# Eight of 22 gate and up pairs of four swiglu FFNs by seven half-size products, inner tiles in four groups

## The chip, the cores and the metric

One core of a Trainium2 chip runs the whole program. The metric is the device time of one execution in microseconds; the median of the runs is compared. TensorE (PE) multiplies, VectorE (DVE) and ScalarE (ACT) evacuate, round and combine, GpSimd (POOL) takes a few sums, and SyncE's queue (SP) starts the weight transfers.

## The reference

Two transformer blocks of 512 tokens and width 1024, in float32. The first block has two layers, and each layer has two swiglu FFNs, so there are four of them:

```
def swiglu(x, w_gate, w_up, w_down):
    return (jax.nn.silu(x @ w_gate) * (x @ w_up)) @ w_down

for i in range(DEPTH):                                  # DEPTH = 2
    h = rmsnorm(x, g_ffn1_pre[i])
    x = x + 0.5 * rmsnorm(swiglu(h, w1_gate[i], w1_up[i], w1_down[i]), g_ffn1_post[i])
    ...                                                 # attention mix
    h = rmsnorm(x, g_ffn2_pre[i])
    x = x + 0.5 * rmsnorm(swiglu(h, w2_gate[i], w2_up[i], w2_down[i]), g_ffn2_post[i])
    ...                                                 # gated projection ("ple")
```

The inner width is 2816, which is 22 tiles of 128. The second block (a recurrent mix, an FFN with a convolution, another gated projection) is not touched.

## The kernel before, in words

Activations lie transposed: a tile has 128 channels on the partitions and 512 tokens in its columns, and the width of 1024 makes eight such tiles (k = 0 to 7). Every product of float32 numbers is made of three matmuls: both operands are split into a high part (a copy rounded to float32r) and a low part (the rest), and `mm3` (L284 to L287) adds high x high, high x low and low x high in PSUM.

Weights arrive as raw buffers of up to 1024 columns, four of them in flight. `prep` (L138 to L150) makes the two parts of one unit: ACT casts 512 columns to `wh` (L146), and DVE subtracts to get `wl` (L147). `run` walks the list of steps that the builder wrote down; in front of each step it prepares at most one unit more, as long as fewer than `wu` units are prepared and not used up (8 in an FFN). So the order of instructions on every engine is fixed by that list, and each engine works through its own queue in order.

An FFN (`ffn`, L658) works inner tile by inner tile. The gate of tile n is eight `mm3` over all 512 tokens into one PSUM bank (24 matmuls of 512 columns), the up half the same into another bank. DVE multiplies each by the row of inverse norms (`act_gate` L681, `act_up` L706), ACT applies Silu (L683), DVE multiplies both (L712), and `split` makes the high and low part of the result, `dh` on ACT (L306) and `dl` on DVE (L307). The inner tiles are taken in pieces of 6, 8 and 8. After a piece the down projection runs over its tiles, for each of the eight output tiles (`pt` in PSUM), and its result is added to `f` (L779). Ahead of every piece but the first the gates of its first two tiles are computed before the down projection of the piece before, so that DVE can finish the last tile meanwhile.

The last piece has no such cover behind it. Its last four output tiles (`tail`) are computed in two halves of 256 tokens, and `boundary` (L501) threads the norm and the next sublayer's inputs through the second halves by a written plan: squares of the sum on ACT, sums over the partitions by PE transposes (`ss` L314), an inverse root on POOL (L323), a broadcast by PE (`bc` L330), then the update of x and the new `hh` and `hl`, with which the next sublayer's first matmuls (`hd` L638) start.

The lines that matter for the bank of a product are these:

```
def ps(self, s="o"):
    return self.pp.tile([P, T], F32, tag="ps", name=self.name(s))
```

A PSUM tile is one bank of 512 columns. Waits between engines are set for a tile as a whole, not for a range of its columns.

## Time and profile before

| what | value |
|---|---|
| three runs | 2878.39, 2880.08 (median) and 2880.47 us |
| profiled execution, its own time | 2879.94 us |
| its span in the trace | 2878.2 us |
| PE busy | 2850.8 us (99%) in 14942 matmuls |
| DVE busy | 1706.4 us (59%) |
| ACT busy | 1250.5 us (43%) |
| POOL busy | 216.9 us (8%) |
| chain that ended last | PE 88%, DVE 7%, ACT 4% |
| mean granted TensorE clock | 0.998 of full speed |
| DMA | 264.30 MB, mean 92 GB/s |

The time of an execution is 1.7 us longer than the span, which counts from the first to the last traced instruction. A busy PE is not PE at its peak: matmuls are pipelined, so the distance from one start to the next tells what one costs, not its duration. A group's row gives how often it ran, its busy time, the mean of one, and the idle time of the engine before it with what ended it.

### The profile page before, as it was taken

What the parts mean: (1) busy time and instruction counts of PE and PEld (TensorE: products, weight loads), DVE (VectorE), ACT (ScalarE), POOL (GpSimd) and SP (SyncE); (2) the same over time, 40 slices, a digit from 0 to 9 for tenths busy, and PEclk for the clock granted to TensorE, in tenths of its full rate; (3) what the DMA queues carried; (4) which work ended last, traced back from release to release, by engine and by line L of the source; (5) the groups of instructions that cost most, each with busy time, mean ns of one, the idle gap of its engine ahead of it and who ended that gap; (6) DMA issues with size and microseconds to landing.
All of it is one profiled execution on the core that took longest, in us unless ns stands there. A gap on an engine that the chain in (4) does not pass through costs nothing.

```text
span 2878.2 us, 38507 instructions
## 1 busy us (share of the span) xinstructions
PE 2850.8 (99%) x14942; PEld 2449.4 (85%) x14946; DVE 1706.4 (59%) x3048; ACT 1250.5 (43%) x2464; POOL 216.9 (8%) x252
## 2 busy tenths in 40 slices
PE   9999999999999999999999999999999999999999
PEld 8888898798888998888987898888988889888888
DVE  6454476865444595434668674434788746735458
ACT  5342347653322364322457653323546635433234
POOL 0000110010000220000111100000400001000013
PEclk9999999999999999999999999999999999999999
DMA  5333321123223223222121223233222222322320
GB/s 178 114 102 96 101 64 54 50 81 110 103 95 110 74 73 125 96 95 97 67 83 56 83 73 108 93 106 99 75 84 95 103 103 80 118 95 96 108 98 30
DMA packets 77750, 264.30 MB, mean 92 GB/s; under 512 B 9088, under 2 KB 11008, under 8 KB 77568
## 3 DMA queue, kind: packets, MB, share of 16 engines
q1 hardware_dynamic: 75600, 259.29, 27.3%
q0 software_dynamic: 1536, 2.10, 0.3%
q8 instruction: 118, 1.93, 0.3%
q10 hardware_dynamic: 432, 0.45, 0.1%
q14 instruction: 64, 0.52, 0.1%
HBM read 257.61 MB, written 2.10 MB: 90 GB/s over the span
## 4 chain that ended last, share of the span: by engine, by line
PE 88%; DVE 7%; ACT 4%; issue 1%; DMA 0%; POOL 0%; SPq 0%; DVEq 0%; ACTq 0%
PE gu L286 13%; PE gu L287 13%; PE gu L285 13%; PE hd L638 9%; PE pt L286 8%; PE pt L287 8%; PE pt L285 8%; PE in L285 3%; PE in L287 3%; PE in L286 3%; ACT p L1391 1%; DVE wl L147 1%; DVE ptl L307 1%; ACT wh L146 1%; DVE p L1400 1%
## 5 line engine op out<-in xcount | busy, mean ns | idle before, releaser
L147 DVE TENSOR_TENSOR wl<-raw,wh 128x512 fp32r<-128x512 f32 (+1 forms) x993 | 643.8, 692 | 149.0 <-ACT wh L146 144.9
L285 PE MATMUL gu<-hh,wh 128*128 128x512 f32 x1632 | 635.9, 390 | 0.0
L287 PE MATMUL gu<-hh,wl 128*128 128x512 f32 x1632 | 635.0, 389 | 0.0
L286 PE MATMUL gu<-hl,wh 128*128 128x512 f32 x1632 | 635.0, 389 | 0.0
L146 ACT CAST wh<-raw 128x512 fp32r<-128x512 f32 (+1 forms) x993 | 545.2, 605 | 202.3 <-PE pt L286 98.2
L285 PE MATMUL pt<-dh,wh 128*128 128x512 f32 (+1 forms) x1056 | 377.7, 358 | 0.0
L286 PE MATMUL pt<-dl,wh 128*128 128x512 f32 (+1 forms) x1056 | 376.9, 357 | 0.0
L287 PE MATMUL pt<-dh,wl 128*128 128x512 f32 (+1 forms) x1056 | 376.8, 357 | 0.0
L287 PEld LDWEIGHTS gu<-hh,wl 128*128 128x128 f32 x1632 | 306.4, 188 | 63.6
L285 PEld LDWEIGHTS gu<-hh,wh 128*128 128x128 f32 x1632 | 306.4, 188 | 63.3
L286 PEld LDWEIGHTS gu<-hl,wh 128*128 128x128 f32 x1632 | 306.4, 188 | 63.2
L306 ACT CAST dh<-ur 128x512 fp32r<-128x512 f32 x112 | 69.5, 620 | 463.1 <-DVE ur L712 463.1
L655 POOL TENSOR_TENSOR acc<-acc,sq 128x256 f32<-128x256 f32 (+1 forms) x96 | 99.6, 1037 | 1916.8 <-ACT sq L653 1916.2
L286 PEld LDWEIGHTS pt<-dl,wh 128*128 128x128 f32 x1056 | 199.6, 189 | 28.9
L285 PEld LDWEIGHTS pt<-dh,wh 128*128 128x128 f32 x1056 | 199.5, 189 | 29.0
L287 PEld LDWEIGHTS pt<-dh,wl 128*128 128x128 f32 x1056 | 199.5, 189 | 28.5
L706 DVE TENSOR_TENSOR ur<-gu,rb 128x512 f32<-128x512 f32 x102 | 70.4, 690 | 253.2 <-PE gu L287 253.2
L779 DVE TENSOR_TENSOR f<-pt,f 128x512 f32<-128x512 f32 (+1 forms) x100 | 58.3, 583 | 237.4 <-PE pt L287 237.3
L285 PE MATMUL in<-hh,wh 128*128 128x512 f32 x432 | 170.6, 395 | 3.9 <-DVE ptl L307 2.3
L638 PE MATMUL hd<-hh,wh 128*128 128x256 f32 (+1 forms) x672 | 170.1, 292 | 0.4 <-ACT hh L464 0.4
L287 PE MATMUL in<-hh,wl 128*128 128x512 f32 x432 | 168.4, 390 | 0.0
L286 PE MATMUL in<-hl,wh 128*128 128x512 f32 x432 | 168.3, 390 | 0.0
(396 smaller groups left out, 4448.4 us busy)
## 6 DMA issues: line engine op xcount, KB each, us to landing
raw<-in_w_dram SPq DMA_DIRECT2D x449, 512.0 KB, 3.3
raw<-in_w_dram SPq DMA_DIRECT2D x36, 384.0 KB, 3.1
x<-in_x_dram SPq DMA_DIRECT2D x8, 256.0 KB, 6.5
raw<-in_w_dram SPq DMA_DIRECT2D x4, 432.0 KB, 3.6
pt<-in_p_dram SPq DMA_DIRECT2D x6, 256.0 KB, 4.0
out_dram<-pgt SPq DMA_DIRECT2D x10, 128.0 KB, 1.7
qh<-qrh POOLq DMA_DIRECT2D x16, 64.0 KB, 1.9
ql<-qrl POOLq DMA_DIRECT2D x16, 64.0 KB, 2.0
```

What stands on the lines that cost most here:

```text
L146: self.S.copy(h, src)
L147: self.low.append((u, lambda h=h, l=l, src=src: self.V.tensor_sub(l, src, h.bitcast(F32))))
L285: self.E.matmul(o, lh, rh, start=start, stop=False, **kw)
L286: self.E.matmul(o, lh, rl, start=False, stop=False, **kw)
L287: self.E.matmul(o, ll, rh, start=False, stop=stop, **kw)
L306: self.S.copy(hi, src)
L307: self.V.tensor_sub(lo, src, hi.bitcast(F32))
L638: self.E.matmul(q, w, h, start=k == 0 and j == 0, stop=k == KD - 1 and j == 2)
L655: eng.tensor_tensor(sub.acc[:, t0:t1], sub.acc[:, t0:t1], sq[:, t0:t1], op=ALU.add)
L706: V.tensor_mul(ur[:, t0:t1], ou, sub.rb[:, t0:t1])
L779: V.tensor_tensor(f, q, f, op=ALU.add)
L1391: S.activation(s.p[t][:, c : c + n], s.sc[t][:, c : c + n], AF.Exp, bias=mx[qb], accum_out=s.sum[:, qb : qb + 1])
```

## The change

In each of the four swiglu FFNs the inner tiles 8 to 11 and 14 to 17 are computed in another way, and the pieces are 6, 6, 6 and 4 tiles instead of 6, 8 and 8. The FFN of the second block stays as it was.

For such a tile the gate weights, the up weights and the normalised input are cut into 2 x 2 blocks: the weights by the upper and lower 512 channels and by gate and up, the input by the upper and lower channels and by tokens 0 to 255 and 256 to 511. Strassen's identity (in Winograd's form) needs seven products of these blocks instead of eight. Each product is four `mm3` over 256 tokens, 12 matmuls of 256 columns.

- Four combinations of the input (`token_sums`, once for each of four channel pairs of an FFN) are made by ACT and DVE during the first piece and kept in 16 tiles.
- Four combinations of the weights are made for each tile by DVE (`prep_part`, lines with q1 to q4), and then rounded and split as other weights are. A tile has four parts: part 0 holds blocks 11 and q1, part 1 holds 12 and q2, part 2 holds q4 and q3, part 3 holds 22. The limit `wu` is 5 parts or units from tile 4 on until tile 18.
- The products go into two banks, `r` (both halves of its columns) and `r3` (one half). `seven_run` writes the steps of a group of four tiles. For tile n they are: two products into `r` (part 0); ACT's copy of `r` (`s15`); a product into `r3` (part 1); then, for the tile before, its last product (part 3) and the steps that finish it; a second product into the first half of `r` (part 1); ACT's copy of that half (`s2`); a product into the second half of `r` (part 2); DVE's addition, scaling and Silu of the gate; another product into the first half of `r` (part 2); DVE's up half.

The first two tiles of a piece stay as they were, and so do their early gates. Cut to its core the diff is:

```diff
-WU_TAIL, WU_SB, WU_MLA = 10, 6, 6
+WU_TAIL, WU_SB, WU_MLA, WU_SEVEN = 10, 6, 6, 5
+SEVEN = (8, 9, 10, 11, 14, 15, 16, 17)
...
+    def prep_part(self, u):
+        q = u.quad
+        ra, rb = (r.tile for r in q.raws)
+        w = {"22": ra[:, 0:T], "11": ra[:, T:], "12": rb[:, 0:T], "21": rb[:, T:]}
+        low = []
+        def add(key, a, b):
+            q.q[key] = self.a("q")
+            self.V.tensor_add(q.q[key], a, b)
+        def put(key, src):
+            h, l = u.blocks[key] = (self.a("wh", F32R), self.a("wl", F32R))
+            self.S.copy(h, src)
+            low.append(lambda: self.V.tensor_sub(l, src, h.bitcast(F32)))
+        if u.j == 0:
+            put("11", w["11"])
+            add("q1", w["21"], w["22"])
+            put("q1", q.q["q1"])
+        elif u.j == 1:
+            put("12", w["12"])
+            add("q2", q.q.pop("q1"), w["11"])
+            put("q2", q.q["q2"])
+        elif u.j == 2:
+            add("q4", q.q.pop("q2"), w["12"])
+            put("q4", q.q.pop("q4"))
+            add("q3", w["11"], w["21"])
+            put("q3", q.q.pop("q3"))
+        else:
+            put("22", w["22"])
...
+        def token_sums(k):
+            g1, g2, x1, x2 = sub.gpre(k), sub.gpre(k + 4), self.X[k], self.X[k + 4]
...
+        def product(o, part, block, key, start):
+            h, l = part.blocks[block]
+            for k in range(4):
+                c = slice(k * P, (k + 1) * P)
+                self.mm3(o, h[:, c], l[:, c], *operand(key, k), start and k == 0, k == 3, skip=True)
...
+            def last(st, n):
+                step(lambda: product(st.r[:, A], st.u[3], "22", "t4", False), [st.u[3]], mm=True)
+                def out():
+                    gr, ur = raw.pop(n)
+                    V.scalar_tensor_tensor(ur[:, A], st.r[:, A], -1.0, gr[:, A], op0=ALU.mult, op1=ALU.mult)
+                    V.tensor_mul(ur[:, B], ur[:, B], gr[:, B])
+                    hid[n] = (self.a("dh", F32R), self.a("dl", F32R))
+                    self.split(ur, *hid[n])
+                    st.r = None
+                step(out)
...
+                def one(st=st):
+                    st.r, st.r3 = self.ps("gu"), self.ps("gu")
+                    product(st.r[:, A], st.u[0], "11", "11", True)
+                    product(st.r[:, B], st.u[0], "q1", "t1", False)
...
+                def gate_b(st=st, n=n):
+                    gr = pair(n)[0]
+                    V.tensor_tensor(gr[:, B], st.r[:, B], st.s2[:, A], op=ALU.add)
+                    V.tensor_mul(gr, gr, sub.rb)
+                    S.activation(gr, gr, AF.Silu)
+                    self.later.append(lambda: V.tensor_mul(gr, gr, sub.rb))
...
+                step(one, [st.u[0]], mm=True)
+                step(copy)
+                step(lambda st=st: product(st.r3[:, A], st.u[1], "12", "21", True), [st.u[1]], mm=True)
+                if prev:
+                    last(*prev)
+                step(lambda st=st: product(st.r[:, A], st.u[1], "q2", "t2", False), [st.u[1]], mm=True)
+                step(two)
+                step(gate_a)
+                step(lambda st=st: product(st.r[:, B], st.u[2], "q4", "22", False), [st.u[2]], mm=True)
+                step(gate_b)
+                step(lambda st=st: product(st.r[:, A], st.u[2], "q3", "t3", False), [st.u[2]], mm=True)
+                step(up_b)
+                prev = (st, n)
+            last(*prev)
...
-                self.ffn(..., (6, 8, 8), 4.0 / D, 4.0 * EPS, first=L == 0)
+                self.ffn(..., (6, 6, 6, 4), 4.0 / D, 4.0 * EPS, first=L == 0, seven=SEVEN)
```

In the functions `copy` and `two`, left out above, ACT copies `st.r` to `st.s` and its first half to `st.s2`; `gate_a` is DVE's addition of `st.r3` and `st.s`, and `up_b` its subtraction for the second half of the up product.

How the order of instructions moves is shown at three places of the first layer's first FFN. The first is DVE at a tile inside the second group. Before, tile 16 (`gr`, `ur`: its gate and up half; `rb`: the inverse norms) takes these rows on DVE:

```order
L681 TENSOR_TENSOR gr_2259<-gu_2193,rb_483 128x512 [waits PE_49]
L147 TENSOR_TENSOR wl_2254<-raw_2109,wh_2253 128x512 [waits DMAHW5_49,Activation_49]
L147 TENSOR_TENSOR wl_2257<-raw_2109,wh_2256 128x512 [waits Activation_49]
L681 TENSOR_TENSOR gr_2267<-gu_2224,rb_483 128x512 [waits PE_49]
L706 TENSOR_TENSOR ur_2260<-gu_2271,rb_483 128x512 [waits PE_49]
L147 TENSOR_TENSOR wl_2297<-raw_2147,wh_2296 128x512 [waits DMAHW6_49,Activation_49]
L147 TENSOR_TENSOR wl_2300<-raw_2147,wh_2299 128x512 [waits Activation_49]
L712 TENSOR_TENSOR ur_2260<-ur_2260,gr_2259 128x512 [waits DVE_49]
L307 TENSOR_TENSOR dl_2303<-ur_2260,dh_2302 128x512 [waits Activation_49]
```

The banks `gu` are read once each, and the weights prepared in between come straight from raw buffers. The same place with the change, from the finish of tile 14 (`ur_2354`) to the gate of tile 15 (`gr_2497`), with `q` the combinations of weights for tile 16:

```order
L863 SCALAR_TENSOR_TENSOR ur_2354<-gu_2279,gr_2353 128x256 [waits PE_49]
L864 TENSOR_TENSOR ur_2354<-ur_2354,gr_2353 128x256
L371 TENSOR_TENSOR dl_2463<-ur_2354,dh_2462 128x512 [waits Activation_49]
L167 TENSOR_TENSOR wl_2458<-raw_2071,wh_2457 128x512
L162 TENSOR_TENSOR q_2481<-q_2424,raw_2311 128x512
L162 TENSOR_TENSOR q_2486<-raw_2195,raw_2311 128x512
L167 TENSOR_TENSOR wl_2484<-q_2481,wh_2483 128x512 [waits Activation_49]
L167 TENSOR_TENSOR wl_2489<-q_2486,wh_2488 128x512 [waits Activation_49]
L890 TENSOR_TENSOR gr_2497<-gu_2396,s_502_2429 128x256
L894 TENSOR_TENSOR gr_2497<-gu_2395,s_514_2491 128x256 [waits PE_49,Activation_49]
L895 TENSOR_TENSOR gr_2497<-gr_2497,rb_483 128x512 [waits DVE_49]
L897 TENSOR_TENSOR gr_2497<-gr_2497,rb_483 128x512 [waits Activation_49]
```

The two combinations for tile 16 (L162) now stand behind the finish of tile 14 (L863), which waits for PE. The second place is ACT at the same tile, from the copy of `r` (L883) to the Silu of tile 15:

```order
L883 COPY s_502_2429<-gu_2395 128x512 [waits PE_49]
L166 CAST wh_2457<-raw_2071 128x512
L370 CAST dh_2462<-ur_2354 128x512 [waits DVE_49,Activation_49]
L166 CAST wh_2483<-q_2481 128x512 [waits DVE_49,Activation_49]
L166 CAST wh_2488<-q_2486 128x512 [waits DVE_49]
L887 COPY s_514_2491<-gu_2395 128x256 [waits PE_49]
L896 ACTIVATE gr_2497<-gr_2497 128x512 [waits DVE_49]
```

Before, ACT had only casts from raw buffers, one `dh` and one Silu in a tile. Now the copy L887 of tile 15 stands behind two casts for tile 16 that wait for DVE. The third place is PE at the same tile, where the product of q2 into `r` (`gu_2395`) ends and the product of q4 into its other half begins:

```order
L350 MATMUL gu_2395<-ts_808,wh_2268 128x256
L351 MATMUL gu_2395<-ts_807,wl_2269 128x256
L349 MATMUL gu_2395<-hh_244,wh_2339 128x256 [waits Activation_49]
L350 MATMUL gu_2395<-hl_245,wh_2339 128x256
L351 MATMUL gu_2395<-hh_244,wl_2340 128x256
```

Before, the 24 matmuls of a gate followed each other with waits only for their weights. Now the product of q4 starts with a wait for ACT, and twelve rows further the product of q3, the next one into `gu_2395`, starts with a wait for DVE. By the counts in the built program the first is that of the copy L887 and the second that of DVE's addition L894.

## Rows read from the trace of the kernel before

**Rows 1.** Page, part 1 and part 4: busy time of each engine, shares of the last chain.
```profile
PE 2850.8 (99%) x14942; PEld 2449.4 (85%) x14946; DVE 1706.4 (59%) x3048; ACT 1250.5 (43%) x2464; POOL 216.9 (8%) x252
...
PE 88%; DVE 7%; ACT 4%; issue 1%; DMA 0%; POOL 0%; SPq 0%; DVEq 0%; ACTq 0%
```

**Rows 2.** Busy time by stretch, first FFN: start:end, length, PE, PEld, DVE, ACT, POOL, clock, DMA.
```profile
60.00:330.00 270.00, 270.00 (x1193) 223.64 (x1192) 134.09 (x228) 87.75 (x159) 1.36 (x5) 1.00 0.34 103
```

**Rows 3.** Timeline, PE: start, duration, line, product; gate matmuls of 512 columns.
```profile
300.05 0.39 PE L286 MATMUL gu<-hl,wh 128*128 128x512 f32 x1
...
302.77 0.39 PE L286 MATMUL gu<-hl,wh 128*128 128x512 f32 x1
```

**Rows 4.** Timeline: down matmuls of 256 columns, and DVE's addition behind one.
```profile
351.77 0.28 PE L285 MATMUL pt<-dh,wh 128*128 128x256 f32 x1
...
358.13 0.28 PE L287 MATMUL pt<-dh,wl 128*128 128x256 f32 x1
...
358.45 0.42 DVE L779 TENSOR_TENSOR f<-pt,f 128x256 f32<-128x256 f32 x1 [2.46 <-PE pt L287]
...
361.01 0.28 PE L287 MATMUL pt<-dh,wl 128*128 128x256 f32 x1
```

**Rows 5.** Timeline, DVE and ACT around one up half of the third FFN piece.
```profile
807.39 0.69 DVE L706 TENSOR_TENSOR ur<-gu,rb 128x512 f32<-128x512 f32 x1 [4.75 <-PE gu L287]
808.00 1.28 DVE L147 TENSOR_TENSOR wl<-raw,wh 128x512 fp32r<-128x512 f32 x2
809.20 0.68 DVE L712 TENSOR_TENSOR ur<-ur,gr 128x512 f32<-128x512 f32 x1
809.97 0.62 ACT L306 CAST dh<-ur 128x512 fp32r<-128x512 f32 x1 [5.64 <-DVE ur L712]
810.50 1.14 ACT L146 CAST wh<-raw 128x512 fp32r<-128x512 f32 x2
810.62 0.69 DVE L307 TENSOR_TENSOR dl<-ur,dh 128x512 fp32r<-128x512 f32 x1 [0.74 <-ACT dh L306]
```

**Rows 6.** Groups by line and shape, whole span: count, busy us, mean ns.
```profile
L560 DVE TENSOR_TENSOR accx<-accx,sq 128x512 f32<-128x512 f32 x49 | 33.9, 691 | 4.4
...
L683 ACT ACTIVATE gr<-gr 128x512 f32<-128x512 f32 x88 | 55.1, 632 | 189.8 <-DVE gr L681 189.7
...
L777 ACT COPY f<-pt 128x512 f32<-128x512 f32 x40 | 23.5, 587 | 102.6 <-PE pt L287 102.6
...
L821 ACT COPY f<-pt 128x256 f32<-128x256 f32 x24 | 8.8, 366 | 24.3 <-PE pt L287 24.3
```

**Rows 7.** Timeline, boundary behind the first FFN: from the last first-half product to the next matmuls.
```profile
361.13 0.38 PE L314 MATMUL ss<-ident,acc 128*128 128x128 f32 x2
...
366.49 0.48 DVE L538 SCALAR_TENSOR_TENSOR t<-f,cols,sb 128x256 f32<-128x256 f32 x1 [0.43 <-ACT sb L523]
...
367.53 0.51 ACT L540 ACTIVATE hh<-x,cols 128x256 fp32r<-128x256 f32 x1 [1.07 <-DVE x L539]
...
374.32 0.51 ACT L540 ACTIVATE hh<-x,cols 128x256 fp32r<-128x256 f32 x1 [1.78 <-DVE x L539]
```

**Rows 8.** Timeline, PE: two waits of PE in the attention of layers 2 and 1.
```profile
1616.12 0.27 PE L287 MATMUL yv<-pth,vl 128*128 128x128 f32 x1
1618.44 0.69 PE L285 MATMUL part<-yh,wh 128*128 128x512 f32 x1 [2.04 <-ACT p L1391]
...
1621.92 0.43 PE L287 MATMUL part<-yh,wl 128*128 128x512 f32 x1
...
574.42 0.50 PE L285 MATMUL part<-yh,wh 128*128 128x512 f32 x1 [1.98 <-ACT p L1391]
574.76 0.39 PE L286 MATMUL part<-yl,wh 128*128 128x512 f32 x1
```

**Rows 9.** Busy time by stretch around the first wait of rows 8; the clock stands third from the end.
```profile
1619.00:1620.00 1.00, 1.00 (x4) 0.81 (x3) 0.18 (x2) 1.00 (x5) 0.00 (x0) 0.50 0.00 0
```

More of the change, by code (lines that the diff above doesn't have):

```diff
@@ L74, in __init__ @@
         self.lo = lambda k: units[k].lo(0)[:, c]
+class Quad:
+    def __init__(self, hosts):
+        self.hosts, self.raws, self.q = hosts, None, {}
+        self.parts = [Part(self, j) for j in range(4)]
+class Part:
+    n, dims = 1024, (8, P)
+    def __init__(self, quad, j):
+        self.quad, self.j, self.blocks = quad, j, {}
 class Raw:
@@ L135, in cols_units @@
         return [Unit(lambda inp, c=c: host(inp, c), (kn, width)) for c in range(c0, c0 + ncol, width)]
+    def prep_part(self, u):
[25 more added lines that the diff above has]
+            put("22", w["22"])
+        self.low.append((u, lambda: [f() for f in low]))
     def prep(self, u):
+        if isinstance(u, Part):
+            return self.prep_part(u)
         kn, w = u.dims
@@ L209, in run @@
         for u in order:
+            if isinstance(u, Part):
+                if u.quad.raws is None:
+                    u.quad.raws = [Raw(), Raw()]
+                    for r, host in zip(u.quad.raws, u.quad.hosts):
+                        block = Unit(host, (8, P))
+                        block.at, r.units, r.n = 0, [block], RAW
+                    raws.extend(u.quad.raws)
+                u.raw = u.quad.raws[1]
+                continue
             if len(raws) < 3 or raws[-1].n + u.n > RAW:
@@ L216, in run @@
             r.left = sum(-(-u.dims[0] // (T // u.dims[1])) for u in r.units)
+        for u in order:
+            if isinstance(u, Part):
+                u.quad.raws[0].left, u.quad.raws[1].left = 4, 3
         self.declare(raws)
@@ L241, in flush_low @@
                     f()
-                    u.raw.left -= 1
-                    if u.raw.left == 0:
-                        self.rlive -= 1
+                    for r in (u.quad.raws[: 2 if u.j < 3 else 1] if isinstance(u, Part) else [u.raw]):
+                        r.left -= 1
+                        if r.left == 0:
+                            self.rlive -= 1
                 else:
@@ L740, in ffn @@
         self.plain_head(sub, head, evac)
+        sums = {}
+        A, B = slice(0, T // 2), slice(T // 2, T)
+        def token_sums(k):
+            g1, g2, x1, x2 = sub.gpre(k), sub.gpre(k + 4), self.X[k], self.X[k + 4]
+            xg, a, b = self.a("xg"), self.a("ta"), self.a("tb")
+            S.activation(xg, x1, AF.Copy, scale=g1)
+            V.tensor_sub(a[:, A], xg[:, A], xg[:, B])
+            V.scalar_tensor_tensor(a[:, B], x2[:, B], g2, xg[:, B], op0=ALU.mult, op1=ALU.subtract)
+            V.scalar_tensor_tensor(b[:, A], x2[:, B], g2, a[:, A], op0=ALU.mult, op1=ALU.add)
+            V.scalar_tensor_tensor(b[:, B], x2[:, A], g2, b[:, A], op0=ALU.mult, op1=ALU.subtract)
+            ah, al, bh, bl = (self.a("ts", F32R) for _ in range(4))
+            self.split(a, ah, al)
+            S.activation(bh, b, AF.Copy, scale=-1.0)
+            V.scalar_tensor_tensor(bl, b, -1.0, bh.bitcast(F32), op0=ALU.mult, op1=ALU.subtract)
+            sums[k] = (ah, al, bh, bl)
@@ new lines, in operand @@
+        def operand(key, k):
+            if key in ("11", "21", "22"):
+                hh, hl = sub.h[k + 4 * (key[0] == "2")]
+                c = A if key[1] == "1" else B
+            else:
+                i = 0 if key in ("t1", "t3") else 2
+                hh, hl = sums[k][i : i + 2]
+                c = A if key in ("t1", "t2") else B
+            return hh[:, c], hl[:, c]
+        def product(o, part, block, key, start):
[3 more added lines that the diff above has]
+                self.mm3(o, h[:, c], l[:, c], *operand(key, k), start and k == 0, k == 3, skip=True)
@@ L751, in body @@
                         self.step(ahead[1])
+                    if seven and n == 4:
+                        wu, self.wu = self.wu, WU_SEVEN
+                    if seven and n > seven[-1]:
+                        self.wu = wu
+                    if n in seven:
+                        if n - 1 not in seven:
+                            seven_run([i for i in seven if n <= i < n0 + kn])
+                        continue
                     if n not in early:
@@ L755, in body @@
                         self.both(item(i, 1))
+                        if seven and pc == 0:
+                            self.step(lambda k=i - 2: token_sums(k))
                 if not final:
```

32 lines of the change are left out of this document (29 added, 3 removed).

## The prediction

> **What bounds the kernel now.** I read the page first: PE is busy for 99% of the span and holds 88% of the chain that ended last, with DVE at 59% and ACT at 43% [rows 1]. Then the stretch that the change rewrites: from 60 to 330 us, inside the first FFN, PE is busy for all of 270 us at full clock, DVE for 134 and ACT for 88 [rows 2]. There PE waits for nobody, so time is won only by fewer or cheaper matmuls, and lost by any wait of PE that nothing covers. The third view is the timeline, for what one matmul costs from start to start. Twelve starts with 512 columns take 302.77 - 300.05 = 2.72 us, 226.7 ns each [rows 3]. With 256 columns 77 starts take 361.01 - 351.77 = 9.24 us, 120.0 ns each [rows 4]. Half the columns cost 53%, not 50%.
>
> **What the products save.** A gate and up pair took 48 matmuls of 512 columns, 48 x 226.7 ns = 10.88 us. Now it takes 84 of 256 columns, 84 x 120.0 ns = 10.08 us. That is 0.80 us, on 8 tiles of 4 FFNs: 32 x 0.80 = 25.7 us. Of eight products one is saved, 12.5%, but the shorter matmul gives 5 points of it back. The last piece of 4 tiles instead of 8 also turns 96 down matmuls of 256 columns into 48 of 512 in each FFN: 96 x 0.120 - 48 x 0.2267 = 0.64 us, 2.6 us in four. Together 28 us. The order agrees with the count: 32 x 36 matmuls more and 4 x 48 fewer make the 960 by which PE's rows grew, so the change does what it says.
>
> By the Trainium skill, "TensorE: Matmul & The Clock Gate", section "Back-to-back issue gap", the distance at full clock is columns / 2.4 plus 2.5 ns, 215.8 and 109.2 ns here; an estimate by that page would save 1.19 us in a pair, 38 us in all instead of 25.7. The trace differs from it, and its 120.0 ns decide.
>
> **What the products cost: waits of PE.** Before, a bank was filled, read once and left. Now bank `r` is filled in five products with reads between them. Two of these reads have nothing between them and the next product into `r`: PE's product of q4 waits for ACT's copy L887, which reads the product just before it, and PE's product of q3 waits for DVE's addition L894, which reads q4's. I walk a tile in the middle of a group, with PE's last product of the tile before ending at 0.
>
> - DVE starts 0.20 us behind the last issue slot of a product (358.13 + 0.12 to 358.45 [rows 4]). DVE's rows of 512 columns follow each other 0.60 us apart and last 0.69, ACT's casts 0.52 apart and last 0.62, and between engines 0.03 to 0.09 pass (all [rows 5]); I take 0.05.
> - L863 runs from 0.20 (0.48 for a three-operand row of 256 columns [rows 7]), L864 from 0.60 to 1.02, `dh` on ACT from 1.07 to 1.69, `dl` from 1.74, `wl` from 2.34, the two sums of weights L162 from 2.94 to 3.63 and 3.54 to 4.23 (0.69 as for other f32 additions [rows 6]).
> - ACT casts q4 from 3.68 to 4.30 and q3 from 4.28 to 4.90, and only then comes the copy L887: 4.80 to 5.17 (0.37 for 256 columns out of PSUM [rows 6]). PE may begin the product of q4 at 5.22. It was done with the product of q2 at 1.44. It waits 3.8 us.
> - Behind q4's product DVE's L894 takes 0.20 + 0.42 + 0.05 = 0.67 us, and PE waits that long for q3.
> - A first matmul behind a wait costs 0.34 us to the next start instead of 0.23 [rows 8]: 0.11, twice.
>
> That makes 4.7 us in a middle tile. From the end of q3's product PE has 5.8 us of products that wait for nothing late, in which DVE (14 rows of 512 and 5 of 256 columns in a tile, 10.4 us) and ACT catch up, so the next tile begins as this one did. A group has two such tiles. In its first tile nothing has to be finished before the sums, but the tile before it still has its split to do; the same walk gives 1.0 for the copy, 0.67 for L894 and three restarts, 2.0 us. In its last tile the casts behind it are of plain weights and need no sums: 1.4 for the copy, 0.9 for L894, and 1.1 more because the last product into `r` follows q3's at once and waits for DVE's up half (sum, scaling, Silu of 0.63 [rows 6], scaling, L900); with restarts 3.7. A group costs 2.0 + 2 x 4.7 + 3.7 = 15.1 us, eight groups 121 us.
>
> The bank is the unit of these waits. The Trainium skill, "PSUM — Partial Sum Buffer", section "PSUM bank collisions raise a hardware error", asks that PSUM be guarded by bank and quadrant rather than by address. By that rule q4's product, which goes to the half that the copy does not read, must wait all the same, as in the sum; guarded by address it would start at 1.44, q3 would wait until 5.22 instead, 2.3 us, and eight groups would cost about 33 us less. No run here shows it.
>
> **The clock.** Behind a wait of 2.04 us in the attention of the second layer eight starts took 1621.92 - 1618.44 = 3.48 us instead of 1.81 [rows 8], at a granted clock of 0.50, the 1.2 GHz level [rows 9]. A wait of 1.98 us in the first layer, with the next start 0.34 us on [rows 8], did not bring it down. Waits of 3.8 us are longer than either, so I count the lower level once for each middle tile, 3.48 - 1.81 - 0.11 = 1.6 us: 16 x 1.6 = 26 us. Bounds: nothing, and the lower level all through the middle tiles (below).
>
> **The last piece.** With four tiles instead of eight its down product reaches the newest `dl` after 10 matmuls, 2.3 us, instead of 22, 5.0 us. From the end of the up half to the end of that `dl` it takes 811.31 - 807.19 = 4.1 us [rows 5], so PE waits 1.9 us that were covered, 7.6 in four FFNs. The second halves that cover the boundary shrink from 8 x 1.44 = 11.5 us to 5.8. From the end of the first halves (358.25) to the first `hh` (368.04) 9.8 us pass [rows 4, 7], part of them spent on waiting for a slot on PE; the sixth `hh` then comes 6.8 us behind the first [rows 7], where PE would want it after 4.8. The cost is between 0 and 5 us a boundary. I take 2, since the slots come earlier too and two of the four have a projection's products as cover: 8 us. Together 16 us, bounds 6 and 28.
>
> **Costed at nothing.** The four `token_sums` of an FFN (3.2 us of DVE each) and the eight more additions to `f` lie in stretches where DVE is busy half the time and weights are prepared five units of 5.4 us ahead; without that cover they would be some 13 us an FFN. A tile's weights still are two transfers of a raw buffer; the buffer of part 3 comes free some 6 us ahead of its next use, and if it came late, the sums L162 would.
>
> **The sum.** 121 + 26 + 16 - 28 = 135 us on the profiled execution's own 2879.9 us (the median of the runs, 2880.08, is the same): **3014 us**.
>
> **Rivals.**
> - *The clock holds.* The waits come as walked, and the trace's wait of 1.98 us without a fall is the rule: 3014 - 26 = 2988 us. 22%.
> - *Bare round trips.* ACT and DVE run ahead, so no copy stands behind a late cast. Then a tile costs 0.62 (0.20 + 0.37 + 0.05) + 0.67 + 0.22 = 1.5 us, 32 of them 48, and the group's last wait 8 x 1.1 = 9: 48 + 9 + 16 - 28 = +45, 2925 us. DVE's 50% in rows 2 speaks for it, the place of L162 behind L863 in its queue against it. 10%.
> - *The clock stays low* in the middle tiles. A matmul then costs 0.43 instead of 0.23 [rows 8], half of the difference with 256 columns: 84 x 0.1 = 8.4 us a tile, 16 x 8.4 = 134 instead of 26: 3122 us. PE is busy two thirds of such a tile, which speaks against it. 6%.
> - *Faster: PE does not wait at q4 and q3.* If the two waits there are met early (by casts done a tile ahead, not by L887 and L894), the columns decide: 16 - 28 = -12, 2868 us. The point is 0.80 us a tile: with less than that for both waits the change wins. The bare round trips alone are 1.5, and the built program's counts are those of L887 and L894. 4%.
>
> **How the numbers follow.** The forecast holds 56%, and 2% lie near no change. A measurement of this kernel can tell about 0.2%, 6 us, from nothing. Faster by more than that 0.04, within it 0.02, slower 0.94. The range takes in the forecast with its bounds (walked waits 15% shorter or longer, 18 us; the last piece 6 to 28; the clock in the first and last tiles too, 26 more) and the case without the clock, and reaches to the upper part of the bare round trips: 2935 to 3070.
>
> **What would show it.** Right: PE in the groups has idle time ended by ACT's copy L887, over 3 us in two tiles of a group, and by DVE's L894, about 0.7 in each; the distance of 256-column matmuls stays at 120 ns at full clock; the clock of a group's stretch is below 1. Wrong: no PE wait on L887 over 1 us, or PE busy through the groups. The forecast fails most easily in the size of the wait before q4, 16 times 3.8 us.

## The result and the profile after

The kernel with the change takes **3057.29 us** (median of 4 runs, 3055.04 to 3063.58), against 2880.27 us before on the same chip: a ratio of **1.0621**, 95% interval 1.0608 to 1.0635. That is 177 us slower, where 134 were predicted; it lies inside the range of 2935 to 3070. The profiled execution of the change has a span of 3056.9 us.

The page of the kernel after, parts 1 and 4 (the lines that answer to [rows 1]), and the clock of part 2 by slices of 76 us:

```profile
PE 2892.4 (95%) x15902; PEld 2519.0 (82%) x15906; DVE 1956.2 (64%) x3560; ACT 1369.0 (45%) x2704; POOL 218.3 (7%) x252
...
PEclk9889999999998999999999999998999999999999
...
PE 79%; DVE 13%; ACT 6%; issue 2%; POOL 0%; DMA 0%; ACTq 0%; DVEq 0%; SPq 0%; POOLq 0%
```

PE has fallen from 99% to 95% busy and from 88% to 79% of the last chain; DVE and ACT took the difference. No engine has become the busiest in PE's place: PE stands still for them in places. The view of waits, PE alone (line, what it waited for, us in total, times, longest), says where:

```profile
PE gu L349 <- ACT s L887: 75.5, 32, 3.6
PE gu L349 <- DVE gr L894: 20.2, 32, 0.9
PE gu L349 <- ACT s L883: 19.1, 1, 19.1
PE ss L378 <- DVE acc L719: 6.3, 4, 1.6
PE gu L349 <- DVE ur L900: 6.1, 8, 0.8
```

Four of these lines are the groups' own: 75.5 + 20.2 + 19.1 + 6.1 = 120.9 us. The first two and L900 were forecast; the third, one wait of 19.1 us, was not. Now the timeline around the beginning of the product of q4 in a middle tile (start, duration, engine, line):

```profile
284.74 0.42 DVE L863 SCALAR_TENSOR_TENSOR ur<-gu,gr 128x256 f32<-128x256 f32 x1 [1.26 <-PE gu L351]
285.59 0.62 ACT L370 CAST dh<-ur 128x512 fp32r<-128x512 f32 x1 [1.83 <-DVE ur L864]
...
285.86 0.28 PE L351 MATMUL gu<-ts,wl 128*128 128x256 f32 x1
...
287.45 0.68 DVE L162 TENSOR_TENSOR q<-q,raw 128x512 f32<-128x512 f32 x1
288.05 0.69 DVE L162 TENSOR_TENSOR q<-raw,raw 128x512 f32<-128x512 f32 x1
288.22 1.17 ACT L166 CAST wh<-q 128x512 fp32r<-128x512 f32 x2 [2.02 <-DVE q L162]
...
289.30 0.37 ACT L887 COPY s<-gu 128x256 f32<-128x256 f32 x1
289.71 0.58 PE L349 MATMUL gu<-hh,wh 128*128 128x256 f32 x1 [3.58 <-ACT s L887]
...
293.23 0.58 PE L349 MATMUL gu<-ts,wh 128*128 128x256 f32 x1 [0.59 <-DVE gr L894]
```

This is the chain of the prediction, row by row: PE waits for a copy of 0.37 us that needs nothing but PE's product of q2, and that copy stands in ACT's queue behind two casts of weight sums, which wait 2.02 us for DVE's additions L162, which stand in DVE's queue behind the previous tile's L863, `dl` and `wl`.

Busy time by stretch (start:end, length, the engines, then the clock third from the end): three of the eight groups, from the first product of a group to its last.

```profile
128.10:213.60 85.50, 51.25 (x337) 48.82 (x336) 56.06 (x104) 28.82 (x52) 0.00 (x0) 0.76 0.18 57
268.30:329.70 61.40, 49.08 (x336) 46.88 (x335) 39.06 (x70) 22.99 (x44) 0.00 (x0) 0.86 0.23 75
1935.00:1992.50 57.50, 45.16 (x336) 43.10 (x336) 39.03 (x70) 22.90 (x44) 0.00 (x0) 0.94 0.25 81
```

The other five groups last 61.1, 61.1, 60.5, 60.2 and 61.1 us; all eight last 508.4, and 510.3 from each group's first matmul to the end of its last issue slot (these windows begin up to 0.3 us late). Their products alone, 8 x 28 x 1.44 us, are 322.6, and the four plain tiles that stood there before were 8 x 4 x 10.88 = 348.2. So the groups cost 510.3 - 348.2 = 162 us net, and 187.7 us over their products. Counted over the starts of PE's matmuls in the trace, these are:

- 120.9 us in 73 waits as listed above.
- 14 us around these waits that the view does not list. It counts a wait from the end of the matmul before, 0.28 us behind that one's start (the row at 285.86), where the next start could have come after 0.12 (both are more at the low clock).
- 11 us of restarts: the first start behind a wait is further from the next than usual.
- 41 us of low clock: 450 starts at a granted clock of 0.50, the 1.2 GHz level, lie 0.21 us apart instead of 0.12.

Smaller differences make up the last 1 us. The remaining 17 of the 178.7 us by which the spans differ lie outside the groups; a run below gives them to the short last piece.

### The profile page after: what moved, and what is told of

The parts are those of the page before. It is cut to its first block, busy times and chain, and to the rows that moved or that the text cites. A ratio compares the mean times of both kernels' runs of the same rounds, so it can differ in the third digit from the quotient of the medians.

```text
span 3056.9 us, 41198 instructions
## 1 busy us (share of the span) xinstructions
PE 2892.4 (95%) x15902; PEld 2519.0 (82%) x15906; DVE 1956.2 (64%) x3560; ACT 1369.0 (45%) x2704; POOL 218.3 (7%) x252
## 4 chain that ended last, share of the span: by engine, by line
PE 79%; DVE 13%; ACT 6%; issue 2%; POOL 0%; DMA 0%; ACTq 0%; DVEq 0%; SPq 0%; POOLq 0%
PE gu L349 12%; PE gu L351 11%; PE gu L350 11%; PE hd L702 8%; PE pt L350 7%; PE pt L351 7%; PE pt L349 7%; PE in L349 3%; PE in L351 3%; PE in L350 3%; DVE wl L198 2%; ACT wh L166 1%; ACT p L1576 1%; DVE wl L167 1%; ACT dh L370 1%
## 5 line engine op out<-in xcount | busy, mean ns | idle before, releaser
L198 DVE TENSOR_TENSOR wl<-raw,wh 128x512 fp32r<-128x512 f32 (+2 forms) x897 | 564.9, 674 | 114.9 <-ACT wh L197 111.0
L349 PE MATMUL gu<-hh,wh 128*128 128x512 f32 (+1 forms) x1504 | 561.3, 373 | 75.5 <-ACT s L887 75.5
L197 ACT CAST wh<-raw 128x512 fp32r<-128x512 f32 (+2 forms) x897 | 477.9, 588 | 181.3 <-DMA raw<-in_w_dram 107.9
L350 PE MATMUL gu<-hl,wh 128*128 128x512 f32 (+1 forms) x1504 | 556.9, 370 | 0.0
L351 PE MATMUL gu<-hh,wl 128*128 128x512 f32 (+1 forms) x1504 | 556.6, 370 | 0.0
L349 PEld LDWEIGHTS pt<-dh,wh 128*128 128x128 f32 x992 | 186.9, 188 | 35.5 <-ACT dh L370 4.3
L350 PEld LDWEIGHTS pt<-dl,wh 128*128 128x128 f32 x992 | 186.9, 188 | 33.5 <-DVE dl L371 2.2
L351 PEld LDWEIGHTS pt<-dh,wl 128*128 128x128 f32 x992 | 186.9, 188 | 31.1
L964 DVE TENSOR_TENSOR f<-pt,f 128x512 f32<-128x512 f32 (+1 forms) x132 | 79.6, 608 | 198.5 <-PE pt L351 198.5
L349 PE MATMUL gu<-ts,wh 128*128 128x256 f32 x512 | 159.6, 312 | 45.4 <-DVE gr L894 20.2
```

The lines of the kernel that those rows point to most:

```text
L197: self.S.copy(h, src)
L198: self.low.append((u, lambda h=h, l=l, src=src: self.V.tensor_sub(l, src, h.bitcast(F32))))
L349: self.E.matmul(o, lh, rh, start=start, stop=False, **kw)
L350: self.E.matmul(o, lh, rl, start=False, stop=False, **kw)
L351: self.E.matmul(o, ll, rh, start=False, stop=stop, **kw)
L964: V.tensor_tensor(f, q, f, op=ALU.add)
```

## The experiments

The theory at this point: PE is held by hand-overs of a PSUM tile with nothing else to do, made long by the order of ACT's and DVE's queues; the lower clock and one unlucky place of the setup come on top. The main rival: DVE has more work in a tile than PE, and the waits are its lag, wherever they show.

### 1. The setup moved

```
-                self.hook(60, [self.setup_late, ..., self.rope_tables, ...])
+                self.hook(44, [self.setup_late, ..., self.rope_tables, ...])
```

The hook puts the masks, rope tables and constants behind a step number of the first FFN. Number 60 lies in the second piece, beside tiles 8 and 9, in both kernels; with the change these two tiles are seven-product ones. The timeline of the kernel before, and then of the changed kernel:

```profile
147.98 0.64 ACT L445 ACTIVATE rope_s<-ang 128x512 f32<-128x512 f32 x1 [14.43 <-DVE ang L437]
```

```profile
143.64 0.63 ACT L509 ACTIVATE rope_s<-ang 128x512 f32<-128x512 f32 x1 [16.64 <-DVE ang L501]
...
150.05 0.62 ACT L370 CAST dh<-ur 128x512 fp32r<-128x512 f32 x1 [2.35 <-DVE ur L776]
...
151.10 0.58 ACT L883 COPY s<-gu 128x512 f32<-128x512 f32 x1
...
151.73 0.58 PE L349 MATMUL gu<-ts,wh 128*128 128x256 f32 x1 [19.12 <-ACT s L883]
```

ACT's sine waits for the tables that DVE computes, 14.43 us before and 16.64 now. Before, PE had no wait there (the first FFN's rows in [rows 2] have PE busy throughout); now the copy L883, for which PE waits, is behind the sine in ACT's queue.

> The rope tables and the other late setup are hooked in earlier, so that they lie beside the down products of the first piece as they did before the change, instead of inside the first group of seven-product tiles. Theory (the tables hold VectorE, and PE waits 19.1 us for the first tile's copy in that group): PE's one long wait goes, time about 3035 us (3030 to 3040, the lower end if the clock in that group also comes back from 0.78 towards the 0.86 of the other groups). Rival (the tables are hidden anyway, and the 19 us come back as waits elsewhere in that group): 3057 us.

Measured: **3033.15 us** (ratio to before 1.0538, 1.0520 to 1.0556), 24 us less. The 19.1 us line has shrunk:

```profile
PE gu L349 <- ACT s L883: 1.0, 1, 1.0
```

The first theory holds. The expectation is wrong in one point: before the change the setup did not lie beside the first down pass (85.6 to 118.3 us in that trace), but in the second piece. In the traces the first group falls from 85.5 to 61.6 us; of these 24 us 21 are waits and the rest is mostly low clock. Against that, the first down pass took 34.5 us now instead of 32.6, because DVE's tables delay its weights. The other seven groups have the same waits as in the changed kernel, 12.3 us each, and are yet 12.5 us shorter together: their low clock is shorter in this execution, the fastest of its four (3026 to 3037 us).

### 2. No weight preparation ahead of the copy

```
+                wu, self.wu = self.wu, 0
                 if prev:
                     last(*prev)
                 ...
                 step(gate_b)
+                self.wu = wu
```

> No weight preparation is issued between the last product of the previous tile and the fourth product's addition, so ScalarE's copy before the fourth product (L887) no longer stands behind casts that wait for VectorE's weight sums; the work is all still done, beside the other products. Queue-order theory: PE's wait before the fourth product falls from 3.5 us to about 0.6 in each of the 16 middle tiles (-47 us), and with it the fall of the clock behind it (up to -60 us): about 2950 us, between 2940 and 3010. Rival, VectorE's rate is the bound (about 12.4 us of chained work in a tile against 10.1 of matmuls): the waits only move to the first product of each tile, and the time stays at 2985 to 3060 us. Rival, the waits come from the products sharing a PSUM tile and not from the queue: no change, 3057 us.

Measured: **3010.44 us** (1.0455, 1.0439 to 1.0471), 47 us less than the change. PE's waits:

```profile
PE gu L349 <- ACT s L883: 42.6, 16, 19.2
PE gu L349 <- DVE gr L894: 18.8, 32, 0.6
PE gu L349 <- ACT s L887: 16.2, 32, 1.0
PE gu L349 <- DVE ur L900: 15.7, 8, 2.0
```

The wait before q4 falls from 75.5 to 16.2 us, half a microsecond each: the order of the queues made it, and not the shared PSUM tile alone. But 33 us come up elsewhere, on the first copy L883 (42.6 instead of 19.1, of which one wait is the setup's) and on L900 (15.7 instead of 6.1). The time lies in the range of the rival, DVE's pace, so both are likely to be at work; how much of the waits is DVE's pace this run does not tell.

### 3. The pieces alone

```
-  ... (6, 6, 6, 4), 4.0 / D, 4.0 * EPS, first=L == 0, seven=SEVEN)
+  ... (6, 6, 6, 4), 4.0 / D, 4.0 * EPS, first=L == 0)
```

> All tiles are plain, eight products each, but the pieces stay at 6, 6, 6 and 4 tiles: the price of the short last piece alone. By the prediction's own terms (16 us of waits, less 2.6 saved): 2893 us; by the waits that the trace of the change shows there (13.5 us, less 2.6): about 2891 us. Rival, the last piece's waits come from the seven-product tiles before it: 2877 to 2880 us.

Measured: **2897.41 us** (1.0062, 1.0047 to 1.0077), 17.3 us over before with no seven-product tile at all. The rival falls. The forecast was 13.4 net; the waits of the last piece are there without the groups:

```profile
367.40 0.44 PE L378 MATMUL ss<-ident,acc 128*128 128x128 f32 x2 [1.61 <-DVE acc L719]
...
379.56 0.39 PE L702 MATMUL hd<-hh,wh 128*128 128x256 f32 x1 [0.81 <-ACT hh L604]
```

With 0.37 us for the broadcast (`bc`) and 0.65 and 0.22 us for `dh` and `dl` these are 3.7 us in the first FFN, and by the view of waits 14 in all four. Less the 2.6 saved that leaves some 6 of the 17.3 us. Some 5 of them are what the view does not list around the 22 waits that came up, 0.24 us each, as in the groups. 162 in the groups and 17 here are the whole difference.

### 4. A product put between q4 and q3

```
-                step(lambda: product(st.r3[:, A], st.u[1], "12", "21", True), ...)
                 if prev:
                     last(*prev)
                 ...
                 step(lambda: product(st.r[:, B], st.u[2], "q4", "22", False), ...)
+                step(add_b)
+                step(lambda: product(st.r3[:, A], st.u[1], "12", "21", True), ...)
+                step(gate_a)
```

> The product that goes to the second PSUM tile (1.22 us of matmuls) stands between the fourth and the third-sum product, so that PE no longer waits there for VectorE's addition (L894, 0.59 us); the long wait for ScalarE's copy (L887) is left as it is. Theory: the low clock behind the long wait lasts 6.5 to 6.8 us here against 3.4 in the attention stretch of the kernel before because a second wait falls into it; without it the low stretch is about 3.4 us, and the time about 3015 us (about 17 us of waits and up to 26 of clock). Rival (the low stretch has its own length whatever follows): only the waits go, about 3040 us. Against both: the first product's copy loses its cover, up to 0.6 us in each of the first tiles (5 us in all).

Measured: **2981.34 us** (1.0353, 1.0338 to 1.0369), 76 us less, which is more than either expected, because the edit did more than it was meant to. Since one weight unit is prepared per step, the moved step also moved the casts of the sums behind the copy:

```profile
273.65 0.36 ACT L887 COPY s<-gu 128x256 f32<-128x256 f32 x1
276.98 1.17 ACT L166 CAST wh<-q 128x512 fp32r<-128x512 f32 x2 [2.97 <-DVE q L162]
```

So the long wait went too, and with it the lower clock. Stretches of the changed kernel and then of this one (busy time by stretch):

```profile
289.00:299.20 10.20, 8.90 (x40) 8.61 (x41) 6.83 (x13) 3.56 (x7) 0.00 (x0) 0.50 0.26 96
293.30:296.90 3.60, 3.60 (x17) 3.60 (x18) 2.60 (x5) 2.11 (x4) 0.00 (x0) 0.50 0.00 0
```

```profile
256.00:310.00 54.00, 45.56 (x346) 43.01 (x345) 39.91 (x75) 25.06 (x48) 0.00 (x0) 1.00 0.31 94
```

Around the end of the wait of 3.58 us the changed kernel's clock is 0.50 for 10.2 us, with 17 starts in 3.6 us; here a whole group runs at 1.00, with waits of up to 2.40. What the run was made for, whether the short wait for L894 by itself prolongs the low clock, it does not tell, since the long wait is gone with it. That stays open.

### 5 and 6. All hand-overs covered, then the old pieces

In words, the new order of the products (n a tile of a group, n+1 the next), and the edit of the sixth run in short:

```
+    one(n+1), q3(n), r3(n+1), q2(n+1), 22(n), q4(n+1)
+    (each copy or addition straight behind its product, ahead of weight preparation; hook at 44)
```

```
-    SEVEN = (8, 9, 10, 11, 14, 15, 16, 17), pieces (6, 6, 6, 4)
+    SEVEN = (8, 9, 10, 11, 16, 17, 18, 19), pieces (6, 8, 8)
+    seven_run(ns, [item(i, 0) for i in (ns[-1] + 1, ns[-1] + 2)])
```

The second also puts the gate products of the two plain tiles behind a group between its last hand-overs.

> Setup hooked early as in the first experiment, and the seven products reordered so that every hand-over of a PSUM tile has at least one product of the other tile in between: one(n+1), q3(n), r3(n+1), q2(n+1), last(n), q4(n+1); the copies and additions are issued straight behind their product, ahead of weight preparation. Pieces unchanged. Theory (the cost is uncovered round trips and queue order): of the 12.3 us of waits in a group at most 1 to 4 are left, no low clock behind them; time 2872 (no waits: before, plus 17 for the pieces, less 25.7 for 32 tiles) to about 2905, most likely 2890. Rival (VectorE's work in a tile, 10.4 us of rows and about 12.4 with what it waits for, paces PE's 10.1): a tile takes 12 us in any order as in the covering experiment, 2950 us.

> The same order, with the pieces of before (6, 8, 8) and the groups at tiles 8 to 11 and 16 to 19, each followed by two plain tiles whose gate products cover the last tile's hand-overs. Theory (the pieces' price of 17 us is independent of the tiles): 15 to 20 us under the run beside it, about 2872, which would be at or under the kernel before. Rival (eight hidden tiles leave too few buffers for weights beside the token sums, so weight preparation comes late and PE waits for it): no gain on the run beside it or a loss, 2890 to 2930 us.

Measured: **2955.88 us** (1.0264, 1.0247 to 1.0281) and **2909.49 us** (1.0102, 1.0087 to 1.0117). The first is what the rival gave (2950) and not what I expected (2890): with at least 1.4 us of products in every gap PE still waits. The second is 46 us better, more than the 17 of the pieces, though not the 2872 us that were expected: with the plain gate products at a group's end PE's waits for L885 and L891 fall from 55.1 us to 27.9, two waits of 1.7 us in a group. The timeline of the sixth run, DVE from one L885 (the addition behind q4) to the next:

```profile
154.39 0.42 DVE L885 TENSOR_TENSOR gr<-gu,s 128x256 f32<-128x256 f32 x1
...
156.23 0.69 DVE L888 TENSOR_TENSOR gr<-gr,rb 128x512 f32<-128x512 f32 x1 [0.70 <-ACT gr L887]
...
163.50 0.69 DVE L371 TENSOR_TENSOR dl<-ur,dh 128x512 fp32r<-128x512 f32 x1 [0.69 <-ACT dh L370]
...
166.69 0.42 DVE L885 TENSOR_TENSOR gr<-gu,s 128x256 f32<-128x256 f32 x1
167.17 0.38 PE L349 MATMUL gu<-ts,wh 128*128 128x256 f32 x1 [1.78 <-DVE gr L885]
```

From 154.39 to 166.69 are 12.3 us, in which DVE is idle only for the 0.70 and 0.69 us that these rows name, both on ACT, and for some 0.3 us in gaps too short to be listed. That leaves 10.6 us of rows and 10.9 with the short gaps. PE's products of a tile take 10.1. **DVE paces the tile**, and no order of PE's products mends that as long as DVE's rows stay; here the order lets two tiles pass before the lag reaches PE. The second piece of the first FFN, four seven-product and four plain tiles, lasts 89.7 us in this run, where eight plain tiles took 87.0:

```profile
121.80:211.50 89.70, 86.25 (x529) 78.03 (x528) 64.00 (x110) 41.75 (x76) 0.00 (x0) 0.98 0.36 114
```

### 7 to 9. Less in DVE's queue, then less on DVE

```
-                step(fn, [u], mm=True)
+                step(fn, [u], mm=True, slot=key not in ("q2", "q4"))
-                self.hook(44, ...)
+                self.hook(self.late_at, ...)
```

```
-                    self.later.append(lambda: V.tensor_mul(gr, gr, sub.rb))
+                    self.later.append(lambda: G.tensor_mul(gr, gr, sub.rb))
-                    self.split(ur, *hid[n])
+                    S.copy(hid[n][0], ur)
+                    G.tensor_sub(hid[n][1], ur, hid[n][0].bitcast(F32))
```

```
-            put("22", w["22"])
+            put("22", w["22"], self.G)
```

> The last kernel (products reordered, pieces 6, 8, 8) with the setup moved to the second down pass, where VectorE is busy 3.8 of 10 us, and no weight preparation issued ahead of the second and fourth products, so that the addition L885, for which PE waits 1.7 us twice in a group, stands behind less work in VectorE's queue. Setup: in the last kernel the first down pass took 36.4 us against 32.6 before, so -4 us. Queue-order theory: the waits (28 us) and the low clock behind them (about 12) go too, 2865 us. Rival (VectorE paces the tile: about 10.9 us busy and 1.4 us idle for ScalarE against 10.1 us of products): the waits stay in other places, 2895 to 2908 us.

> As the kernel beside it, with two of VectorE's rows of each seven-product tile (the second multiplication of the gate, L888, which waits 0.7 us for ScalarE, and the low part of the hidden tile, which waits 0.7 us too) given to GpSimd, which does nothing there and took 1.46 us for a row of that size. Theory (VectorE's pace): its tile falls from 12.3 to about 9.7 us, under PE's 10.1, so no waits in the groups: before less 25.7, about 2855 us (2850 to 2870). Rival (the queue's order alone counts): no change on the run beside it. Rival (GpSimd's rows slow VectorE's, or come late for the down pass): slower than the run beside it.

> As the second kernel, with the low part of the seventh product's weights on GpSimd too: VectorE's tile about 9.1 us. If VectorE's pace still costs waits in the second kernel, these shrink and the time falls by up to 10 us; if there were none left, no change (within 3 us); if PE comes to wait for GpSimd's row (1.5 us), some us slower.

Measured: **2905.17** (1.0090, 1.0075 to 1.0105), **2909.53** (1.0108, 1.0091 to 1.0124) and **2918.80 us** (1.0138, 1.0123 to 1.0153). In all three the new place of the setup was wrong: PE waits for a copy behind it in the second group.

```profile
PE gu L349 <- ACT s L874: 12.5, 1, 12.5
```

With the clock behind it that is some 15 us in each (the seventh run's third piece lasts 92.3 us, the sixth's 78.9, and its second is 2.0 shorter), so the three can be compared with each other, and the first, with the setup somewhere free, would be near 2890 by this estimate. Clearing the queue moved the waits (to L891, L878 and less of L885, 2.4 to 2.8 us in a group instead of 3.5) but not away: a little of the queue, mostly DVE's pace, as in the rival. Giving DVE's rows to GpSimd should then have helped, and did not. The timeline of the eighth run, GpSimd and DVE:

```profile
147.75 1.29 POOL L899 TENSOR_TENSOR dl<-ur,dh 128x512 fp32r<-128x512 f32 x1 [5.20 <-ACT dh L898]
148.05 1.53 DVE L886 TENSOR_TENSOR gr<-gr,rb 128x512 f32<-128x512 f32 x1
...
150.33 1.29 POOL L888 TENSOR_TENSOR gr<-gr,rb 128x512 f32<-128x512 f32 x1 [1.29 <-ACT gr L887]
150.79 1.38 DVE L167 TENSOR_TENSOR wl<-raw,wh 128x512 fp32r<-128x512 f32 x1 [1.21 <-ACT wh L166]
```

A DVE row that comes up while a GpSimd row runs takes 1.4 to 1.5 us instead of 0.69. Groups by line and shape (count, busy us, mean ns), the seventh run and then the eighth:

```profile
L167 DVE TENSOR_TENSOR wl<-raw,wh 128x512 fp32r<-128x512 f32 x96 | 66.0, 687 | 30.7 <-ACT wh L166 30.7
...
L886 DVE TENSOR_TENSOR gr<-gr,rb 128x512 f32<-128x512 f32 x32 | 22.1, 692 | 1.1
```

```profile
L167 DVE TENSOR_TENSOR wl<-raw,wh 128x512 fp32r<-128x512 f32 x96 | 93.9, 978 | 63.0 <-ACT wh L166 63.0
...
L886 DVE TENSOR_TENSOR gr<-gr,rb 128x512 f32<-128x512 f32 x32 | 29.0, 905 | 1.1
```

64 rows of 0.60 us left DVE, 38 us; the rows that stayed grew by 27.9 + 6.9 = 35 us. DVE got almost nothing back, and its idle time for ACT's casts before L167 grew too, from 30.7 to 63.0 us. The ninth run, with a third row on GpSimd, is slower still. The second rival of the eighth run holds. The Trainium skill, "SBUF — State Buffer", section "SBUF: two separate sides", says that a DVE instruction with two SBUF inputs and a GpSimd instruction that reads SBUF exclude each other for a whole instruction; the rows agree: 1.38 and 1.53 us against 0.69, both ending about 0.55 us behind the end of the GpSimd row that they met.

### 10 to 12. Groups of two

```
-    SEVEN = (8, 9, 10, 11, 16, 17, 18, 19)
+    SEVEN = (8, 9, 12, 13, 16, 17)
+    ns = [n, n + 1]
```

The eleventh run adds tiles 20 and 21, with the up products of 18 and 19 as cover. The twelfth is the tenth with the setup at tile 18.

> The reordered kernel with pieces 6, 8, 8 and all rows back on VectorE, but groups of two tiles (8 and 9, 12 and 13, 16 and 17 of 22), each closed by two plain gate products of 5.44 us; the setup at the end of the second piece's tiles. Theory (VectorE needs 12.3 us for a tile that gives PE 10.1, and the lag of about 2.2 us a tile is what PE waits for from the third tile on; plain tiles let VectorE catch up): no waits in the groups, 24 tiles at 0.80 us saved: 2860 us (2858 to 2872). Rival (each entry into a group costs about 2 us whatever its length): 12 entries, 2880 to 2890 us. Rival (the setup collides again): up to 20 us on top.

> As the kernel beside it, with tiles 20 and 21 as a fourth group of two, covered by the up products of tiles 18 and 19. Theory: 8 tiles more, 6.4 us less: 2854 us, if the last tile's sums (about 3 us behind its last product) lie beside the first 4.8 us of the down products. Rival (token sums kept to the end of the piece leave too few buffers for weights, or the last tile is late for the down pass): 2 to 5 us lost in each of four blocks, 2862 to 2880 us.

> As the kernel with three groups of two, with the setup moved once more, to tiles 18 to 21, which are plain and behind the last group of that FFN. In the run before it PE waited 5.2 us for ScalarE's copy in the first FFN's third piece, where ScalarE stood behind the rope tables, and the clock was low for 6.8 us behind it (3.4 lost). Theory: both go, 8 to 9 us under it: 2862 us (2859 to 2866). Rival (the setup costs PE as much beside plain tiles, or comes late for the mixer): no change, 2870 us.

Measured: **2870.51 us** (0.9972, 0.9962 to 0.9981), **2878.50 us** (1.0001, 0.9992 to 1.0009) and **2882.89 us** (1.0014, 1.0005 to 1.0023). The tenth run beats the kernel before, by 8 us. The only wait that the view still lists in any of its twelve groups, and the second piece of the first FFN:

```profile
PE gu L349 <- ACT s L874: 5.2, 1, 5.2
```

```profile
118.40:202.80 84.40, 84.40 (x529) 76.42 (x528) 56.37 (x97) 35.27 (x65) 0.00 (x0) 1.00 0.33 107
```

PE is busy for all of 84.4 us, at full clock, where the same eight tiles took 87.0 before (205.30 - 118.26 in the trace of before): 0.66 us saved in each of four seven-product tiles. That confirms DVE's pace: two tiles' lag is taken up by the plain tiles. 24 tiles save 15.8 us. The one wait, with the clock behind it, gives back 7.2: the third piece of the first FFN lasts 82.0 us instead of 76.2, and its two tiles saved 1.3. That makes -8.6, against -8.0 measured. The wait is once more the setup's.

The eleventh expected 6 us less and cost 8 more: the tiles at the end of the last piece make the down pass wait for `dh` and `dl` (3.3 + 0.9 us in four FFNs) and PE wait for the copy L874 in four groups (5.1 us together); less what the eight tiles save that is 4, and the rest of the 8 us is not located. The twelfth expected the setup to be free beside plain tiles, and it was not: there DVE's tables, 17 us in one piece, hold up the last hidden tiles, and the down pass waits.

```profile
334.06 0.79 PE L349 MATMUL pt<-dh,wh 128*128 128x512 f32 x1 [9.75 <-ACT dh L370]
...
341.96 0.79 PE L349 MATMUL pt<-dh,wh 128*128 128x512 f32 x1 [5.96 <-ACT dh L370]
```

A place of the setup that costs nothing with groups of two was not found; the first part of the second piece, where it lay before, was not tried with them.

## Why the prediction was right, and where its terms were not

The direction, the mechanism and the range were right; the sum was 43 us short, about 20 for the setup, 15 for the clock, 5 for the waits and 4 for the last piece. That the range still held it is in part luck, since the setup stands in no term of it. Step by step:

- **What the products save**, 28 us. The distance of 120.0 ns holds in the changed kernel (rows 0.12 us apart). In the tenth run, with one listed wait in its twelve groups, a tile saves 0.66 us instead of 0.80. Of the 0.14 us that are missing 0.12 lie in two starts of each group of two, like those shown here, which are 0.26 and 0.22 us from the next instead of 0.12: PE is a little too early for DVE's L885, by too little for the view of waits. So the term had the right size, and the tenth run is not quite without waits.

```profile
140.68 0.28 PE L351 MATMUL gu<-hh,wl 128*128 128x256 f32 x1
140.94 0.39 PE L349 MATMUL gu<-ts,wh 128*128 128x256 f32 x1
```

- **Waits of PE**, 121 us with restarts. Measured in the prediction's terms, from the last issue slot and with restarts: 126 us without the setup's (101.8 by the view). By tile, in the view's figures, which leave out 0.16 us of each wait, and without restarts: the first 0.76 + 0.59 = 1.35 where 1.0 + 0.67 was walked; a middle one 3.58 + 0.59 where 3.8 + 0.67 was; the last 1.22 + 0.74 + 0.75 = 2.7 where 1.4 + 0.9 + 1.1 was. The walk through the queues was right to a few tenths in each step. The second run shows its cause, the casts ahead of L887, by taking them away.
- **The bank as the unit.** PE's product of q4 does wait for the copy of the other half; what a guard by address would have done was not tried.
- **The clock**, 26 us: **this term failed** in its size, 41 us measured. Sixteen falls of 1.6 us were taken from a low stretch of 3.5 us [rows 8, 9]. Here the low stretches at the sixteen middle tiles last 10.2 us (four), 6.8 (ten) and 3.4 (one), and one tile has none; 3.5 of the 41 us belong to the first tile of the first group, behind the setup's wait. The second wait of 0.59 us, which falls into the low stretch and which the row of before did not have, does not settle the length by itself, since every middle tile has it. In the first run the same pairs of waits came with 6.8 us (ten), 3.4 (four) and none (two), 28 us in all. What decides it stays open.
- **Costed at nothing.** The setup is missing from this list, and **that step failed**: it lay beside tiles 8 and 9, the change makes these seven-product tiles, and 19.1 us of wait appeared, 24 with what follows it, as the first run shows. `token_sums` and the additions to `f` are indeed hidden: none of PE's waits ends at them.
- **The last piece**, 16 less 2.6. Measured alone in the third run: 17.3 net, inside the bounds. By the view, the waits for `dh` and `dl` were less than walked, 3.5 us in four FFNs instead of 7.6, and the boundaries' were 10 where 8 were taken.

With the measured terms the sum is -28 + 126 + 41 + 20 + 20 = 179 us, and the spans differ by 178.7; the fourth term is the setup's wait, the fifth the last piece without what it saves.

Of the rivals, *the clock holds* and *bare round trips* fell with the rows at 0.50 and the waits of 3.5 us. *The clock stays low* had the right direction, less far. *Faster* named the right point, less than 0.80 us of wait a tile, but not the way to it: waits that are met early are had only where plain tiles give DVE time, as in the tenth run. I wrote that DVE and ACT catch up within a tile. In the changed kernel they do, since its middle tiles last 14.7 us and more; the sixth run, with the long waits gone, shows DVE with 10.9 us of work and 1.4 of waits against PE's 10.1. The prediction's 10.4 us for DVE's rows in a tile was already more than PE's 10.08, and I did not draw the conclusion.

## What to carry to other kernels

When an algorithm trades one product in eight for sums, write the work per tile of every engine beside the new product time first: an engine that was at half load on average may exceed the new tile, and then an order of the products makes the waits shorter but does not end them; here only tiles of the old kind in between did. When PE waits for a short copy, look at what stands ahead of that copy in its engine's queue, and what that waits for. And whatever ran hidden beside the tiles that change has to be costed anew: here the setup, in the same place as before, alone cost 24 of 177 us.

## What the runs showed of the hardware that was not expected

- **The same waits came with low clocks of very different length.** Before, behind 2.04 us of waiting, a low stretch was 3.5 us long [rows 8]. In the changed kernel the granted clock was 0.50, the 1.2 GHz level, for 10.2 us around the end of one wait of 3.58 us with a second of 0.59 us behind it (the row 289.00:299.20 above), and 1.00 throughout behind another such pair, shown here. Shorter waits show no order either: in the sixth run a wait of 1.78 us was followed by a low stretch of 3.4 us, in the fourth run one of 2.40 us by none. So from the waits alone these runs do not tell whether the clock falls, or for how long.

```profile
1956.42 0.39 PE L349 MATMUL gu<-hh,wh 128*128 128x256 f32 x1 [3.58 <-ACT s L887]
```

```profile
1956.40:1971.20 14.80, 10.67 (x85) 10.27 (x85) 10.88 (x20) 6.02 (x11) 0.00 (x0) 1.00 0.22 75
```

- **An idle GpSimd is no spare VectorE for rows out of SBUF**: a row of 0.60 us moved to it took 1.29 us there, and cost the rows that stayed 0.55 us on average (35 us for 64 rows).
